# One-core hybrid-attention layer: in the last phase, the transposed copies of u and y of its last tiles made by DMA transposes instead of TensorE

## The chip, the cores and the metric

The kernel runs on one core of one Trainium2 chip. The metric is the device time of one execution in microseconds (us). The kernel before has a median of 2243.91 us over three runs. A core has TensorE (PE, matrix products), VectorE (DVE), ScalarE (ACT), GpSimd (POOL) and SyncE (SP), which issues nearly all the transfers (DMAs) of this kernel, in order.

## The reference

The reference is one layer of a streaming encoder: 2048 prompt rows and 8 running streams with 16 rows each (128 sample rows, with 512 cached positions). What matters here is the end of the layer.

```
h = rms_norm(x, g) * (1 + scale) + shift
qa, ka, va, za, qb, kb, vb, zb, ga, gb = split(h @ w_in)
oa = differential attention(qa, ka, va);  ob = stick-breaking attention(qb, kb, vb)
u  = [rms_norm(oa) * silu(za),  ob * silu(zb)]
y  = sigmoid(ga) * (u_a @ w_branch_a) + sigmoid(gb) * (u_b @ w_branch_b)
x  = x + gate * (y @ w_out)
out = rms_norm(x, final_g)
```

All matrices are 1024 wide (u_a and u_b 512 each). The gate is one row for the whole prompt and one row for each of the 8 sample streams.

## The kernel before

The rows are 17 tiles of 128: 16 of the prompt and one of the sample (number 16, `NT`). Every float32 operand of a product is split into a high and a low float16 part, and a product is the sum of three float16 products (high by high, high by low, low by high).

A first part normalizes x and projects, eight head units follow with their attention over all tiles, and the last phase computes u, y and the output tile by tile. The change touches the last phase alone. Its loop runs over slots n = 0 to 18, in the order `tiles` = 0 to 14, the sample, 15; places in this order are called indices here, so index 15 is the sample tile and index 16 the last prompt tile. In slot n the kernel emits:

- `branches` of index n: four pieces (two column halves, two branches) of 12 products each (L1463). DVE multiplies each result by its sigmoid gate (L1465) and adds the two branches (L1468); ACT and DVE write y as two float16 halves into the single buffer `y16` (L1469, L1470).
- `output` of index n-1: two halves of 24 products each with w_out (L1492). DVE scales by the gate (L1496), POOL adds to x (L1500). For the sample tile the gate rows are first loaded and spread over the partitions by a product (`gate_rows`, L1449 and L1451), and ACT and DVE scale (L1498, L1499).
- `inputs` of index n+2: loads (L1290, L1291, L1297), u, and its split into `u16`, which lies in `hs[2]` (L314, L319).
- `turned` of index n+1 and `turned_y` of index n: the products need u and y with their columns on the partitions. `transposed` does that: 16 transposes of 128x128 on TensorE (L1280) into two PSUM banks, and two copies to SBUF by ACT (L1281), one for each half.
- `normed_rows` and `stored_rows` of index n-2: the sum of squares (ACT, L294), the reciprocal root by ten small DVE operations (`rsqrt_one`, L273 to L286), the scaling by final_g (DVE, L1510) and the store (L1511).

Beside the first 13 slots (`S_TILES`) runs the attention of the sample tile (`sample`, `aside`), whose products with cached values are L871, with keys L848, and whose weights are already turned by DMA transposes (L614). A list of positions in each slot (`IN_AT`, and the numbers in `side`) and the costs of the pieces set where each piece is emitted; a scheduler then fixes the order on every engine. Cached values lie in the four buffers `dc`.

## Time and profile before

| | |
|---|---|
| Median of 3 runs | 2243.91 us (2241.89 to 2244.5) |
| Profiled execution, its own time | 2241.22 us |
| Its span | 2239.4 us |
| PE busy | 2082.9 us (93%) |
| DVE busy | 1749.2 us (78%) |
| ACT busy | 1621.5 us (72%) |
| POOL busy | 704.0 us (31%) |

The profile is of one execution. Its own time is 1.8 us above its span. Matmuls are pipelined, and their ends are modelled, so the time of one matmul in a chain is read from start to start and not from its duration. "L1280" is line 1280 of the kernel before. A row of the timeline has the start, the length, the engine, the line, the operation with its operands and count, and in brackets the idle time before it and what ended it. In the answers by stretches, each engine has its busy time and, in brackets, its number of instructions.

### The profile page before, as it was taken

The page shows a single profiled execution, that of the slowest core. Times are in us where ns is not written, and L with a number is a line of the kernel's source. Part 1 is how long each engine was busy: PE and PEld are TensorE (multiplying, and loading weights), DVE is VectorE, ACT ScalarE, POOL GpSimd, SP SyncE. Part 2 cuts the span into 40 slices and gives each one's busy share as a digit, 9 for nine tenths or more (in the row PEclk, how much of TensorE's full clock was granted, in tenths as well). Part 3 has the DMA queues.
Part 4 walks back from the last instruction along what each step waited for, and adds up shares of the span by engine and source line. Part 5 has one row for each costly group of instructions (what it writes and reads, how often), then busy time and mean ns, then how long its engine had stood idle before and what let it go on. Part 6 is the DMA issues. An engine that isn't in the chain of part 4 may idle for free.

```text
span 2239.4 us, 41736 instructions
## 1 busy us (share of the span) xinstructions
PE 2082.9 (93%) x14752; PEld 1127.2 (50%) x14752; DVE 1749.2 (78%) x3795; ACT 1621.5 (72%) x3228; POOL 704.0 (31%) x610
## 2 busy tenths in 40 slices
PE   5998999999999999999989998999998679999997
PEld 3654555555555555555555554555554334444543
DVE  4657868889886788988778888886688868788863
ACT  3967877789877677988677788866677665766641
POOL 1123014456410443742034365402234412212211
PEclk7999999999999999999999999999998799999999
DMA  9777668889796989979879899666677899999521
GB/s 331 266 238 184 165 152 212 196 221 205 197 247 160 224 201 201 213 205 225 200 197 211 182 234 223 170 157 136 140 157 158 183 259 255 235 255 240 158 101 57
DMA packets 805827, 445.30 MB, mean 199 GB/s; under 512 B 537354, under 2 KB 744506, under 8 KB 805104
## 3 DMA queue, kind: packets, MB, share of 16 engines
q1 hardware_dynamic: 804668, 442.24, 79.6%
q8 instruction: 115, 1.88, 0.3%
q14 instruction: 96, 0.79, 0.1%
q10 hardware_dynamic: 948, 0.39, 0.1%
HBM read 228.82 MB, written 86.02 MB: 141 GB/s over the span
## 4 chain that ended last, share of the span: by engine, by line
PE 31%; DVE 7%; ACT 5%; DMA 5%; issue 3%; POOL 1%; SPq 0%; DVEq 0%; POOLq 0%; ACTq 0%
PE ps_o L1492 7%; PE ps_mm L1463 7%; PE ps_mm L460 5%; PE ps_t L536 5%; DMA wt<-sc_n 2%; DVE sc_n L670 2%; PE ps_s L1280 1%; PE ps_s L697 1%; PE ps_s L696 1%; ACT sc_p L130 1%; POOL sc_p L676 1%; PE ps_o L757 1%; PE ps_t L871 1%; ACT sc_n L130 1%; DVE sc_n L607 1%
## 5 line engine op out<-in xcount | busy, mean ns | idle before, releaser
L676 POOL TENSOR_TENSOR sc_p<-sc_p,sc_n 128x127 f32<-128x127 f32 (+7 forms) x192 | 313.1, 1633 | 668.0 <-DVE sc_n L670 515.5
L460 PEld LDWEIGHTS <-hs 128*128 128x128 f16 x3120 | 292.6, 99 | 315.3 <-issue 6.7
L460 PE MATMUL ps_mm<-wa,hs 128*128 128x512 f16 x1590 | 383.3, 380 | 3.3 <-DMA hs<-hT_d 2.1
L460 PE MATMUL ps_mm<-wb,hs 128*128 128x512 f16 x1530 | 382.3, 381 | 0.2 <-DVE qbuf L495 0.2
L536 PE MATMUL ps_t<-wb,hs 128*128 128x512 f16 x1224 | 291.9, 379 | 3.2 <-DVE qst L564 2.9
L670 DVE TENSOR_TENSOR_SCAN sc_n<-ps_s,sc_n,zero_t 128x512 f32<-128x512 f32 x192 | 245.5, 1279 | 35.5 <-ACT ps_s L130 30.1
L696 PE MATMUL ps_s<-k,qst 128*128 128x512 f16 (+3 forms) x640 | 225.7, 354 | 33.5 <-DVE sc_n L670 24.8
L607 DVE TENSOR_TENSOR sc_n<-sc_p,sc_n 128x128 f16<-128x128 f32 (+7 forms) x192 | 221.9, 1158 | 40.0 <-ACT sc_n L604 39.5
L536 PEld LDWEIGHTS <-hs 128*128 128x128 f16 x1632 | 154.8, 98 | 182.2 <-DVE qst L564 7.3
L130 ACT ACTIVATE sc_p<-ps_s,usc 128x512 f32<-128x512 f32 (+3 forms) x320 | 202.9, 634 | 37.6 <-PE ps_s L697 23.0
L697 PE MATMUL ps_s<-k,qst 128*128 128x512 f16 (+3 forms) x640 | 226.1, 354 | 0.0
L604 ACT CAST sc_n<-sc_p 128x128 f16<-128x128 f32 (+7 forms) x192 | 154.8, 807 | 64.7 <-POOL sc_p L676 64.0
L130 ACT ACTIVATE ps_s<-ps_s,usc 128x512 f32<-128x512 f32 (+3 forms) x320 | 195.1, 610 | 0.0
L1492 PE MATMUL ps_o<-wo,wb 128*128 128x512 f16 x816 | 186.7, 385 | 0.7 <-ACT wb L1281 0.7
L757 PE MATMUL ps_o<-v,wt 128*128 128x128 f16 x1088 | 136.1, 227 | 21.8 <-DMA wt<-sc_n 21.8
L1500 POOL TENSOR_TENSOR x<-m,x 128x512 f32<-128x512 f32 x34 | 49.9, 1467 | 272.6 <-DVE m L1496 164.9
L590 DVE TENSOR_SCALAR_CACHE_REDUCE sc_p<-ps_s,usc 128x512 f32<-128x512 f32 (+3 forms) x160 | 106.3, 665 | 32.5 <-PE ps_s L697 18.6
L757 PEld LDWEIGHTS <-wt 128*128 128x128 f16 x1088 | 103.6, 102 | 50.0 <-DMA wt<-sc_n 27.0
L758 PE MATMUL ps_o<-v,wt 128*128 128x64 f16 x1088 | 128.6, 199 | 0.0
L1492 PEld LDWEIGHTS <-wb 128*128 128x128 f16 x816 | 79.6, 99 | 97.1 <-issue 4.6
L670 DVE TENSOR_TENSOR_SCAN sc_n<-ps_s,zero_t 128x128 f32<-128x128 f32 (+3 forms) x128 | 104.2, 815 | 22.9 <-ACT ps_s L130 22.1
L501 POOL TENSOR_TENSOR rot<-pr,rope 128x256 f32<-128x256 f32 x68 | 56.8, 835 | 203.8 <-ACT pr L474 115.1
(370 smaller groups left out, 4572.2 us busy)
## 6 DMA issues: line engine op xcount, KB each, us to landing
hs<-hT_d SPq DMA_DIRECT2D x130, 512.0 KB, 4.8
g_d<-gt SPq DMA_DIRECT2D x68, 256.0 KB, 3.1
out_dram<-pr SPq DMA_DIRECT2D x204, 64.0 KB, 3.6
wa<-in_w_in_dram SPq DMA_DIRECT2D x34, 256.0 KB, 5.3
o_d<-o SPq DMA_DIRECT2D x136, 64.0 KB, 2.0
wa<-g_d SPq DMA_DIRECT2D x17, 512.0 KB, 4.7
wb<-g_d SPq DMA_DIRECT2D x17, 512.0 KB, 4.8
hs<-o_d SPq DMA_DIRECT2D x17, 512.0 KB, 4.2
```

The source lines that it names most:

```text
L130: i = S.activation(**kw)
L460: T.matmul(box["p"], box["h"][:, hi, k, :], U["w"][k][:, wi, :], start=(n == 0), stop=(n == 3 * KT - 1))
L536: T.matmul(box["g"][:, 0:gw], box["h"][:, hi, k, :], U["wg"][k // per][:, k % per, wi, :], start=(j == 0), stop=(j == 3 * KT - 1))
L604: x = S.copy(out=hi, in_=src)
L607: V.tensor_tensor(out=lo, in0=src, in1=hi, op=ALU.subtract)
L670: V.tensor_tensor_scan(out=dst[:, lo : lo + n][:, ::-1], data0=src[:, 0:n][:, ::-1], data1=zero_t[:, 0:1].to_broadcast([P, n]), initial=fi ...
L676: G.tensor_tensor(out=p[:, 0:m], in0=p[:, 0:m], in1=n[:, 1 : m + 1], op=ALU.mult)
L696: T.matmul(p[:, 0:n], qst[:, c, :], kk[:, c, 0:n], start=True, stop=False)
L697: T.matmul(p[:, 0:n], qst[:, 2 + c, :], kk[:, c, 0:n], start=False, stop=not diag)
L757: T.matmul(po[:, c * P : (c + 1) * P], wt[:, wj, :], vt[:, c, :, :], start=first, stop=False)
L1463: T.matmul(pb, st["u"][:, ui * 8 + br * 4 + k, :], wb[br * 4 + k // 2 * 2 + j][:, wi, k % 2, :], start=(n == 0), stop=(n == 11))
L1492: T.matmul(po, st["y"][:, yi * 8 + k, :], wo[j * 4 + k // 2][:, wi, k % 2, :], start=(n == 0), stop=(n == 3 * KT - 1))
```

## The change

A constant `MOVED = 12` marks the indices from which the transposes move.

- u of indices 12 to 16 is turned by one DMA transpose from `u16` (SP issues it), instead of 16 TensorE transposes and two ACT copies.
- y of indices 12 to 15 is turned by one DMA transpose from `y16` into a new buffer `yT`, taken from the four `dc` buffers. It is emitted right after the last branch piece (position 4.4 in place of 7). y of index 16 is still turned by TensorE.
- The sample's gate rows are loaded once (9 x 1024) in slot 15, into a `dc` buffer, and the spreading product stands ahead of the products of each half.
- For the last tile, DVE in place of POOL adds to x, the sum of squares is taken by halves right after each half, and the scaling and the store are done by halves. In the last two slots the rows of index n-2 are normalized at earlier positions.

```diff
+MOVED = 12
...
-    def turned(st):
+    def turned(st, moved=False):
         st["u"] = st["u"].bitcast(F16).rearrange("p (k n) -> p k n", n=P)
+        if moved:
+            nc.sync.dma_start_transpose(out=st["u"], in_=st["u16"].rearrange("p f n -> p (f n)"))
+            return
         for half in range(2):
             transposed(st["u16"], st["u"], half)
...
+        def rows_of_gates():
+            L["gsm"] = dec.tile([P, NB, P], F32, tag="dc", name="gsm", bufs=4).rearrange("p b n -> p (b n)")
+            load(out=L["gsm"][0:9, :], in_=gate_d)
...
-        def turned_y(st):
+        def turned_y(st, moved):
+            if moved:
+                yT = dec.tile([P, NB, P], F32, tag="dc", name="yT", bufs=4).rearrange("p b n -> p (b n)")
+                st["y"] = yT = yT.bitcast(F16).rearrange("p (k n) -> p k n", n=P)
+                nc.sync.dma_start_transpose(out=yT, in_=L["y16"].bitcast(F16))
+                return
...
+                if t == NT:
+                    pg = bank("ts"[j])
+                    T.matmul(pg, sel[0:9, :], L["gsm"][0:9, c], start=True, stop=True)
...
-                    V.tensor_tensor(out=m, in0=m, in1=gate_rows(1, j), op=ALU.mult)
-                G.tensor_tensor(out=x[:, c], in0=m, in1=x[:, c], op=ALU.add)
+                    V.tensor_tensor(out=m, in0=m, in1=pg, op=ALU.mult)
+                if t != tiles[-1]:
+                    G.tensor_tensor(out=x[:, c], in0=m, in1=x[:, c], op=ALU.add)
+                    return
+                V.tensor_tensor(out=x[:, c], in0=m, in1=x[:, c], op=ALU.add)
+                if j == 0:
+                    box["acc"] = tiny.tile([P, 4], F32, tag="mx", name="facc")
+                sum_squares(x[:, c], 512, box["acc"][:, j : j + 1])
...
         def normed_rows(t, box):
+            if t == tiles[-1]:
+                return
...
+            if t == tiles[-1]:
+                r = rsqrt_one(add_up(box["acc"], 2), D, tiny, "rF")
+                for c in (slice(0, 512), slice(512, D)):
+                    V.scalar_tensor_tensor(out=x[:, c], in0=x[:, c], scalar=r, in1=fg[:, c], op0=ALU.mult, op1=ALU.mult)
+                    load(out=y_rows(t)[:, c], in_=x[:, c])
+                return
...
-                side += [(2, lambda n=n: turned(states[tiles[n + 1]])), ...
-            if n > 1:
+                side += [(2, lambda n=n: turned(states[tiles[n + 1]], n + 1 >= MOVED)), ...
+            if n <= NT and tiles[n] == NT:
+                side.append((3.3, rows_of_gates))
+            if n > NT:
+                side += [(0.6, lambda n=n: normed_rows(tiles[n - 2], boxes[n - 2])), (1.1, lambda n=n: stored_rows(tiles[n - 2], boxes[n - 2]))]
+            elif n > 1:
...
-                side.append((7, lambda n=n: turned_y(states[tiles[n]])))
+                side.append((4.4 if MOVED <= n < NT else 7, lambda n=n: turned_y(states[tiles[n]], MOVED <= n < NT)))
```

Ahead of slot 11 the order is the same on every engine. Three places are shown. The lines of the changed kernel are its own (L1298 there is L1297 before, L1346 the transpose of u, L1487 that of y).

The first is SP in slots 12 and 13, before: the gate loads (`g_d`, L1297), the store and load of x (L1511, L1485), and the loads for the inputs (L1290, L1291).

```order
L1297 DMA wa_175<-g_d_110 128x2x512
L1511 DMA out_dram<-x_26237 128x1024
L1291 DMA hs_181<-z_d_95 128x1024
L1485 DMA x_26866<-in_x_prompt_dram 128x1024
L1297 DMA wb_1428<-g_d_110 128x2x512
L747 DMA o_d_78<-o 128x128
L1290 DMA hs_180<-o_d_78 128x1024
L1291 DMA hs_181<-z_d_94 128x512
L1297 DMA wa_169<-g_d_112 128x2x512
```

The same place in the changed kernel:

```order
L1298 DMA wa_175<-g_d_110 128x2x512
L1541 DMA out_dram<-x_26216 128x1024
L1292 DMA hs_181<-z_d_95 128x1024
L1498 DMA x_26793<-in_x_prompt_dram 128x1024
L1298 DMA wb_1428<-g_d_110 128x2x512
L1487 DMA_TRANSPOSE yT<-wa_174 128x16x128
L1346 DMA_TRANSPOSE wb_1432<-hs_182 128x16x128
L748 DMA o_d_78<-o 128x128
L1291 DMA hs_180<-o_d_78 128x1024
L1292 DMA hs_181<-z_d_94 128x512
```

The two transposes stand right behind the second gate load, and ahead of the store of the sample's last head and the loads that follow it.

The second is DVE after the products of the sample's output, before: the sample's scaling (L1499), that of the last tile (L1496), and the start of the sample's reciprocal root.

```order
L1499 TENSOR_TENSOR m<-m,ps_t 128x512 x2
L1496 SCALAR_TENSOR_TENSOR m<-ps_o,fuy,gate 128x512 x2
L273 TENSOR_SCALAR r_27575<-facc 128x1
L276 TENSOR_SCALAR r_27575<-r_27575 128x1
L278 TENSOR_SCALAR rF<-r_27575 128x1
L280 SCALAR_TENSOR_TENSOR r_27575<-rF,r_27575 128x1
```

The same place in the changed kernel (L1512 is L1496 before, L1519 the new addition on DVE, L274 is L273 before):

```order
L1515 TENSOR_TENSOR m<-m,ps_t 128x512
L1515 TENSOR_TENSOR m<-m,ps_s 128x512
L1512 SCALAR_TENSOR_TENSOR m<-ps_o,fuy,gate 128x512
L1519 TENSOR_TENSOR x_27345<-m,x_27345 128x512
L274 TENSOR_SCALAR r_27381<-facc 128x1
L277 TENSOR_SCALAR r_27381<-r_27381 128x1
L1512 SCALAR_TENSOR_TENSOR m<-ps_o,fuy,gate 128x512
L279 TENSOR_SCALAR rF<-r_27381 128x1
L1519 TENSOR_TENSOR x_27345<-m,x_27345 128x512
L281 SCALAR_TENSOR_TENSOR r_27381<-rF,r_27381 128x1
```

The second half of the last tile now stands between the first operations of the sample's root.

The third is the end of DVE, before: the sample's last scaling, and then the last tile's root and scaling.

```order
L1510 SCALAR_TENSOR_TENSOR x_27426<-x_27426,rF,gt_1421 128x1024
L273 TENSOR_SCALAR r_27592<-facc 128x1
L276 TENSOR_SCALAR r_27592<-r_27592 128x1
L278 TENSOR_SCALAR rF<-r_27592 128x1
L280 SCALAR_TENSOR_TENSOR r_27592<-rF,r_27592 128x1
L281 TENSOR_SCALAR r_27592<-r_27592 128x1
L282 TENSOR_SCALAR r_27592<-r_27592 128x1
L283 TENSOR_TENSOR rF<-rF,r_27592 128x1
L284 SCALAR_TENSOR_TENSOR r_27592<-rF,r_27592 128x1
L285 TENSOR_SCALAR r_27592<-r_27592 128x1
L286 TENSOR_TENSOR rF<-rF,r_27592 128x1
L1510 SCALAR_TENSOR_TENSOR x_27514<-x_27514,rF,gt_1421 128x1024
```

The same place in the changed kernel:

```order
L277 TENSOR_SCALAR r_27427<-r_27427 128x1
L287 TENSOR_TENSOR rF<-rF,r_27381 128x1
L279 TENSOR_SCALAR rF<-r_27427 128x1
L1540 SCALAR_TENSOR_TENSOR x_27261<-x_27261,rF,gt_1421 128x1024
L281 SCALAR_TENSOR_TENSOR r_27427<-rF,r_27427 128x1
L282 TENSOR_SCALAR r_27427<-r_27427 128x1
L283 TENSOR_SCALAR r_27427<-r_27427 128x1
L284 TENSOR_TENSOR rF<-rF,r_27427 128x1
L285 SCALAR_TENSOR_TENSOR r_27427<-rF,r_27427 128x1
L286 TENSOR_SCALAR r_27427<-r_27427 128x1
L287 TENSOR_TENSOR rF<-rF,r_27427 128x1
L1536 SCALAR_TENSOR_TENSOR x_27345<-x_27345,rF,gt_1421 128x512 x2
```

Three operations of the last tile's root now stand ahead of the sample's scaling, and the last scaling is two halves.

On PE, 144 of the transposes of L1280 are gone from slots 11 to 16.

More of the change, by code (lines that the diff above doesn't have):

```diff
@@ L1543, in layer_kernel @@
             if n + 1 <= NT:
-                side += [(2, lambda n=n: turned(states[tiles[n + 1]])), (4.5, lambda n=n: opened(states[tiles[n + 1]]))]
-            if n > 1:
+                side += [(2, lambda n=n: turned(states[tiles[n + 1]], n + 1 >= MOVED)), (4.5, lambda n=n: opened(states[tiles[n + 1]]))]
+            if n <= NT and tiles[n] == NT:
[3 more added lines that the diff above has]
+            elif n > 1:
                 side += [(1, lambda n=n: normed_rows(tiles[n - 2], boxes[n - 2])), (2.5, lambda n=n: stored_rows(tiles[n - 2], boxes[n - 2]))]
             if n <= NT:
-                side.append((7, lambda n=n: turned_y(states[tiles[n]])))
-            order = [(i, 0, cost, fn) for i, (cost, fn) in enumerate(work)] + [(at - 0.5, i + 1, 0.9 if at in (2, 7) else 0.1, fn) for i, (at, fn) in enumerate(side)]
+                side.append((4.4 if MOVED <= n < NT else 7, lambda n=n: turned_y(states[tiles[n]], MOVED <= n < NT)))
+            order = [(i, 0, cost, fn) for i, (cost, fn) in enumerate(work)] + [(at - 0.5, i + 1, 0.9 if at == 7 or at == 2 and n + 1 < MOVED else 0.1, fn) for i, (at, fn) in enumerate(side)]
             work = [(cost, fn) for _, _, cost, fn in sorted(order, key=lambda e: e[:2])]
```

## Prediction

> **What bounds the kernel now.** I read the head of the page first, then the busy times in the stretches of the last slots (about one slot each), then TensorE's timeline.
>
> ```profile
> span 2239.4 us, 41736 instructions
> ...
> core 0: us, PE busy (x) PEld busy (x) DVE busy (x) ACT busy (x) POOL busy (x), PEclk, DMA share, GB/s
> 2100.00:2124.00 24.00, 24.00 (x222) 11.96 (x221) 18.19 (x39) 14.64 (x21) 5.60 (x5) 1.00 0.51 153
> 2124.00:2147.00 23.00, 23.00 (x140) 11.63 (x137) 14.89 (x32) 10.60 (x15) 4.87 (x3) 1.00 0.24 85
> 2147.00:2169.00 22.00, 22.00 (x123) 10.71 (x121) 15.92 (x42) 12.68 (x17) 3.81 (x3) 1.00 0.44 161
> 2169.00:2192.00 23.00, 23.00 (x139) 11.65 (x138) 11.50 (x23) 6.88 (x9) 2.53 (x2) 1.00 0.15 53
> 2192.00:2216.00 24.00, 23.27 (x124) 10.88 (x120) 9.49 (x21) 6.53 (x10) 2.01 (x2) 1.00 0.12 45
> 2216.00:2239.40 23.40, 11.69 (x50) 4.83 (x50) 8.72 (x25) 3.17 (x5) 4.30 (x4) 0.82 0.11 46
> ```
>
> TensorE is busy for the whole of each stretch up to 2192, at full clock, while DVE has 6 to 12 us to spare in each, ACT 9 to 16, and the transfer engines are busy for about half of their time or less. So in these slots the time is the sum of what TensorE does, and whatever leaves TensorE's list shortens the run, as long as nothing that it then needs comes late. Only the last stretch differs: its products end at 2227.7, and 11.7 us of other work follow.
>
> **The transposes that leave TensorE.** Its timeline, at two places with transposes (L1280) and at the last tile:
>
> ```profile
> 2168.94 1.06 PE L1280 MATMUL ps_s<-id,wa 128*128 128x128 f16 x16
> 2169.83 5.34 PE L1463 MATMUL ps_mm<-wa,wa 128*128 128x512 f16 x24
> ...
> 2182.60 9.01 PE L1492 MATMUL ps_o<-wo,wb 128*128 128x512 f16 x41
> 2191.45 1.06 PE L1280 MATMUL ps_s<-id,wa 128*128 128x128 f16 x16
> 2192.34 5.34 PE L1463 MATMUL ps_mm<-wa,wb 128*128 128x512 f16 x24
> ...
> 2213.06 0.22 PE L1280 MATMUL ps_s<-id,wa 128*128 128x128 f16 x1
> 2213.21 1.12 PE L1451 MATMUL ps_t<-gsm,sel 9*128 9x512 f32 x2
> 2214.26 1.01 PE L1280 MATMUL ps_s<-id,wa 128*128 128x128 f16 x15
> 2216.01 5.79 PE L1492 MATMUL ps_o<-wo,wb 128*128 128x512 f16 x26 [0.74 <-ACT wb L1281]
> 2221.73 1.12 PE L1451 MATMUL ps_t<-gsm,sel 9*128 9x512 f32 x2
> 2222.78 4.92 PE L1492 MATMUL ps_o<-wo,wb 128*128 128x512 f16 x22
> ```
>
> A group of 16 transposes takes from its start to the next start 2169.83 - 2168.94 = 0.89 us, and again 2192.34 - 2191.45 = 0.89. Five u (indices 12 to 16) and four y (12 to 15) are moved, nine groups: 9 x 0.89 = 8.0 us. All nine stand in slots 11 to 16, which the table covers but for slot 11, and there TensorE is never idle. Their 18 copies on ACT go too; ACT has room, so I count nothing for them.
>
> The Trainium skill (TensorE: Matmul & The Clock Gate, Part 4: PE-mode transpose) gives a transpose as about 275 ns in a kernel's context. By that, nine groups would be an estimated 39.6 us. The rows here have 56 ns from start to start, so the trace decides, and the sum has 8.0.
>
> **The transfers that replace them.** Transposes of the same make are in this kernel already. I take their rows from the page's list of transfers (count, median us from issue to landing), from the answer on their line (issue time on SP in ns, minimum, median, maximum, and the times to landing), and the rows around one y.
>
> ```profile
> wt<-sc_n SPq DMA_TRANSPOSE x288, 4.3
> dwt<-dsc SPq DMA_TRANSPOSE x12, 4.2
> ...
> L614 SPq DMA_TRANSPOSE wt<-sc_n x288: 1167/1765/5597, 149.5 to 1770.9; - x144
> DMA to landing us min/median/max: 2.3/4.3/7.6
> ...
> 2139.74 2.75 PE L1463 MATMUL ps_mm<-wb,wa 128*128 128x512 f16 x12
> 2145.64 0.69 DVE L1470 TENSOR_TENSOR wa<-wb,wa 128x512 f16<-128x512 f32 x1 [0.68 <-ACT wa L1469]
> 2146.65 0.53 SPq L1297 DMA_DIRECT2D wb<-g_d  x1
> 2151.80 0.32 SPq L1290 DMA_DIRECT2D hs<-o_d  x1
> ```
>
> A product of 512 columns takes (2191.45 - 2182.60) / 41 = 0.216 us. The tightest y is that of index 13. Its last branch product ends 12 x 0.216 = 2.6 us after 2139.74, at 2142.3, and its float16 halves are ready at 2146.3, 4.0 us later. In TensorE's new order, 15 output products of index 12 and 36 branch products of index 14 come between that last branch product and the first product that reads this y: 51 x 0.216 = 11.0 us. So 7.0 us are left. SP first issues the gate load that waits for the same DVE operation (0.53 us), and 6.5 us remain for a transfer that takes 4.3 in the median: on time by 2.2 us. The longest of the 288 rows, 7.6, would be late by 1.1. The other y have more (61 products instead of 51 for indices 12 and 14; about 14 us and an early y for 15). I take lateness 0, with 1.5 us as the upper end for all four together.
>
> The u are turned a whole slot before their use (some 21 us), and cost TensorE nothing. On SP, the nine issues take 9 x 1.8 = 16 us in all, spread over six slots. Queued behind a waiting y transpose are the store of the sample's last head and the loads of o, z and the next gates. Those feed u of the slot after the next: L1290 at 2151.80 loads what is multiplied one slot later. A delay of 2 to 4 us there is covered by that slot. The new wait of the next `y16` write (ACT) for the transfer to have read the buffer falls near the same 11 us, and holds up ACT and then DVE by a microsecond at most; two product banks are free of it.
>
> In slots 11 and 12 TensorE also serves the sample's attention, whose products wait for ACT, DVE and transfers. Two of the nine groups (u of 12 and 13) leave there. If that chain sets the pace, their 1.8 us return as waits. The new order puts output products ahead of the sample's products where the transposes were, so I take 0 here and 1.8 as the upper end.
>
> **The last tile.** The products of the sample's gate rows stay (1.05 us each, twice), only elsewhere. Before, the copy that TensorE waits for (L1281) stood behind ACT's L1498, which waited for the gate product: from 2213.06 to 2216.01 are 2.95 us, less 1.05 of gate product 1.9. After, it is 0.45 us for the first eight transposes, then ACT's L1498 (0.69) and one copy (1.0), 1.8 with the hops: 0.1 us gained. The work behind the last product is on these rows (the last two are times to landing, of the 512 KB store from the answer on x, and of the smallest store from the page).
>
> ```profile
> 2227.81 0.75 DVE L1496 SCALAR_TENSOR_TENSOR m<-ps_o,fuy,gate 128x512 f32<-128x512 f32 x1 [2.93 <-PE ps_o L1492]
> 2228.64 1.26 POOL L1500 TENSOR_TENSOR x<-m,x 128x512 f32<-128x512 f32 x1 [2.42 <-DVE r L273]
> 2229.93 1.06 ACT L294 ACTIVATE junk<-x 128x1024 f16<-128x1024 f32 x1 [3.78 <-POOL x L1500]
> 2230.90 0.19 ACT L294 ACTIVATION_READ_ACCUMULATOR junk<-x 128x1 f32 x1
> 2231.22 1.28 DVE L1510 SCALAR_TENSOR_TENSOR x<-x,rF,gt 128x1024 f32<-128x1024 f32 x1
> 2234.56 1.28 DVE L1510 SCALAR_TENSOR_TENSOR x<-x,rF,gt 128x1024 f32<-128x1024 f32 x1
> ...
> DMA to landing us min/median/max: 2.6/2.6/2.6
> ...
> o_d<-o SPq DMA_DIRECT2D x136, 64.0 KB, 2.0
> ```
>
> Before, the last scaling ends 2235.84 - 2227.7 = 8.1 us after the last product. DVE was held by the sample's root and scaling until 2231.22 + 1.28 = 2232.5, so the long way over POOL and ACT (to 2231.1) was hidden. After, DVE's order is: scaling (0.75), one step of the sample's root, the addition (0.7), then the sum of squares of half a tile on ACT (about 0.7 with reading, half of 1.06 plus 0.19), which ends 2.4 us after the last product. From there DVE still has the small sum, the rest of the sample's root mixed with the first three steps of the last (seven operations of 0.2, since ten of them lie between 2232.5 and 2234.56), the sample's scaling (1.2), seven steps (1.5) and two halves (1.4): 2.5 + 1.4 + 1.2 + 1.5 + 1.4 = 8.0. So the sample's scaling still lies on the path and almost nothing is gained there. The last store has half the size: between 2.0 and 2.6 us to landing, I take 2.3. Together 0.4 us, and between 1.0 lost (two stores and the sample's share the transfer engines) and 1.2 gained.
>
> **The sum.** 8.0 + 0.1 + 0.3 = 8.4 us off the profiled execution's 2241.22, which makes 2232.8. That execution is 2.7 us under the median of the runs (2243.91); on the median it is 2235.5. The ends: 8.4 - 1.5 (late y) - 1.0 (stores) = 5.9, and 8.4 + 0.9 = 9.3, so 2234.6 to 2238.0, and the runs shown lie 2.0 below to 0.6 above their median: 2232.5 to 2238.6.
>
> **The rivals.** One bound on what can be told: the measurement of this kernel separates about 0.2%, 4.5 us, from no change.
>
> *Partly given back.* The sample's chain keeps slots 11 and 12 at their length, and y of indices 13 and 14 come late. 8.4 - 1.8 - 1.5 - 1.0 = 4.1, 2239.8 on the median, at the border of what can be told. For it speaks that in the first stretch DVE is at 18.19 of 24 us, and that a gate load of 128 x 1024 values goes into the same queue right ahead of each y. Against it that the lateness needs the longest landing of 288, in slots where the transfers are far less busy than where those were taken.
>
> *TensorE was not the bound in these slots.* Then only the end moves, 0.4 us: 2243.5. Against it is the idle time of zero in five stretches.
>
> *Slower: y comes so late that the clock falls.* The place is the first product of `output` in slots 13 to 16. These rows of stretches show what a stall does to the clock (the column before the last two). Behind the last product, which ends at 2227.7, it is full up to 2231 and then half; after an earlier stall it is still half while TensorE is busy again for 4 us, and then full.
>
> ```profile
> 2230.00:2231.00 1.00, 0.00 (x0) 0.00 (x0) 0.85 (x5) 1.00 (x2) 0.00 (x0) 0.99 0.00 0
> 2231.00:2232.00 1.00, 0.00 (x0) 0.00 (x0) 0.94 (x2) 0.08 (x1) 0.00 (x0) 0.50 0.00 0
> ...
> 1776.00:1780.00 4.00, 3.75 (x31) 2.74 (x29) 3.22 (x9) 2.61 (x4) 1.58 (x2) 0.50 1.03 342
> 1780.00:1784.00 4.00, 4.00 (x19) 1.78 (x18) 3.96 (x9) 0.73 (x1) 2.33 (x1) 0.95 0.74 173
> ```
>
> A y late by 3.3 us costs 3.3 and about 2 more for 4 us at half clock, 5.3; four times 21, less 8.4: slower by 12.8, 2256.7. It decides from a mean lateness of 3.2 us for the four (12.9 us of waiting, to be 4.5 above before), so from landings of about 10 us for index 13 and more for the rest. Behind a gate load on the same transfer engines that could be; the longest of 288 is 7.6. The Trainium skill (TensorE: Matmul & The Clock Gate, Part 1) says that the clock halves after one idle window of 3.4 us and takes as long to return; this trace agrees, with the fall between 3.3 and 4.3 us after the last product.
>
> **How the numbers follow.** The forecast has 0.74, partly given back 0.12, not the bound 0.05, slower 0.09. The first is faster by over 0.2% (below 2239.4), the second in something over half of its cases: 0.81 faster. The rest of the second and the third make 0.10 within 0.2%, and 0.09 slower. The range is the forecast's ends and the partial case: the upper end at 2240.5, just over its 2239.8, the lower at 2231.5, 1 us below the forecast's own end, since the sum of start-to-start times has an error of that size.
>
> **What would show it.** Right: the chain of waits runs through PE without a gap from 2100 to the last product; only 32 starts of L1280 are left from slot 12 on; slots 13 to 15 are 1.8 us shorter each; the y transposes land 3 to 6 us after their issue; and the work behind the last product takes 11 to 12 us. Wrong: idle time at the first output product of a slot with a DMA named as what ended it, clock at 0.50 in slots 13 to 16, products with cached values (L871) waiting in slots 11 and 12, or over 12.5 us behind the last product.

## The result, and the profile after

The changed kernel has a median of 2236.94 us (2228.43 to 2245.64) over 22 runs, the kernel before 2243.8 (2235.05 to 2250.03) over 22 runs: a ratio of 0.997, with a 95% interval of 0.996 to 0.9981. That is 6.9 us less by the medians; 8.4 were forecast. The profiled execution took 2238.37 us (before 2241.22).

A line number of the changed kernel is one above that of before up to L1346. After it, the branch products are L1471 (L1463 before), the halves of y L1478, the output products L1508 (L1492), the scaling by the gate L1512 (L1496) and the scaling by final_g L1540. New are the transposes by transfer L1346 (u) and L1487 (y), for the sample tile the product of the gate rows L1503, and in the last tile DVE's addition L1519 and the scaling by halves L1536. The sample's products with cached values are L872.

The first fence has the busy times by stretch of the kernel before, now cut exactly at the slots 11 to 15 (a slot starts with the transposes of the y before it, or with its first branch product). The second has the same of the changed kernel.

```profile
2073.41:2099.24 25.83, 25.83 (x198) 12.90 (x194) 23.31 (x58) 17.33 (x26) 5.16 (x3) 1.00 0.52 170
2099.24:2123.93 24.69, 24.69 (x233) 12.53 (x230) 18.62 (x40) 15.40 (x22) 6.34 (x5) 1.00 0.51 154
2123.93:2146.43 22.50, 22.50 (x132) 11.15 (x130) 14.68 (x30) 10.37 (x14) 4.87 (x3) 1.00 0.25 88
2146.43:2168.94 22.51, 22.51 (x129) 11.19 (x128) 16.13 (x43) 12.85 (x19) 3.81 (x3) 1.00 0.43 157
2168.94:2191.45 22.51, 22.51 (x130) 11.16 (x129) 11.21 (x22) 6.94 (x9) 2.53 (x2) 1.00 0.16 55
```

```profile
span 2236.6 us, 41454 instructions
...
2077.31:2102.69 25.38, 25.38 (x181) 11.85 (x178) 22.80 (x59) 15.69 (x24) 5.23 (x3) 1.00 0.66 199
2102.69:2127.28 24.59, 24.04 (x216) 11.68 (x213) 19.58 (x41) 13.78 (x20) 6.85 (x5) 1.00 0.65 175
2127.28:2148.01 20.73, 20.73 (x101) 9.38 (x99) 12.53 (x30) 5.84 (x10) 4.88 (x3) 1.00 0.54 145
2148.01:2169.91 21.90, 20.89 (x97) 9.32 (x96) 16.80 (x43) 9.48 (x14) 4.25 (x3) 1.00 0.72 191
2169.91:2190.63 20.72, 20.72 (x97) 9.41 (x96) 11.02 (x22) 4.06 (x6) 2.54 (x2) 1.00 0.56 131
```

Slots 13 and 15 are 1.77 and 1.79 us shorter, two groups of transposes each. Slot 14 is only 0.61 shorter, and slots 11 and 12 together 0.55 instead of 1.78. In slots 12 and 14 PE's busy time is below the length. The chain of waits and PE's timeline name what it waited for:

```profile
PE ps_o L1508 <- DMA yT<-wa: 1.0, 1, 1.0
PE ps_o L1508 <- ACT wb L1282: 0.8, 1, 0.8
PE ps_t L872 <- DVE v16c L320: 0.5, 1, 0.5
...
2120.46 0.63 PE L872 MATMUL ps_t<-v16c,dwt 128*32 128x128 f16 x32
2121.59 0.41 PE L872 MATMUL ps_t<-v16c,dwt 128*32 128x128 f16 x16 [0.49 <-DVE v16c L320]
...
2153.19 2.75 PE L1471 MATMUL ps_mm<-wb,wb 128*128 128x512 f16 x12
2156.95 2.55 PE L1508 MATMUL ps_o<-wo,yT 128*128 128x512 f16 x11 [1.01 <-DMA yT<-wa]
...
2213.67 1.06 PE L1281 MATMUL ps_s<-id,wa 128*128 128x128 f16 x16
2215.51 10.53 PE L1508 MATMUL ps_o<-wo,wb 128*128 128x512 f16 x48 [0.79 <-ACT wb L1282]
```

The y of index 13 comes 1.01 us late in slot 14, and a half of the sample's values (L320) 0.49 late in slot 12. The answer on the buffer of the y transposes, and SP's rows around the late one, show why the first happens:

```profile
L1487 SPq DMA_TRANSPOSE yT<-wa x4: 3170/4192/5262, 2124.1 to 2186.4; - x4
...
DMA to landing us min/median/max: 6.1/6.3/6.5
...
2149.01 0.53 SPq L1298 DMA_DIRECT2D wb<-g_d  x1
2149.59 5.26 SPq L1487 DMA_TRANSPOSE yT<-wa  x1
```

The four transposes take 3.2 to 5.3 us to issue. A landing is on record for two of them only, those of indices 12 and 14 (6.1 and 6.5 us). The late one, of index 13, has none: from its issue at 2149.59 to the first product that reads it at 2156.95 are 7.4 us. The forecast had 1.8 and 4.3.

The end, on DVE:

```profile
2228.63 0.16 DVE L304 TENSOR_REDUCE col<-facc 128x1 f32<-128x2 f32 x1
...
2229.32 1.28 DVE L1540 SCALAR_TENSOR_TENSOR x<-x,rF,gt 128x1024 f32<-128x1024 f32 x1
...
2232.05 1.41 DVE L1536 SCALAR_TENSOR_TENSOR x<-x,rF,gt 128x512 f32<-128x512 f32 x2
```

The last product ends at 2215.51 + 10.53 = 2226.04 and the last scaling at 2233.46, 7.4 us behind it (8.1 before). From there to the end of the span are 3.1 us (before 2239.4 - 2235.84 = 3.6). Together 1.1 us are gained behind the last product.

All kernels are the same up to slot 11, but its start varies between 2073 and 2089 us from one execution to another, before any of the changed code. In the profile of the changed kernel it is 3.9 us later than in that of before, which is why these two executions differ by only 2.9 us. So differences below some microseconds are read from the slots, in this table (us). "Tail" runs from the first of the last tile's 48 output products to the end of the span (of before, less the gate product of 1.05 that lies in it). "Rest" is slot 16 up to there, less the gate products in it.

| kernel | slot 11 | 12 | 13 | 14 | 15 | rest | tail |
|---|---|---|---|---|---|---|---|
| before | 25.83 | 24.69 | 22.50 | 22.51 | 22.51 | 23.51 | 22.34 |
| changed | 25.38 | 24.59 | 20.73 | 21.90 | 20.72 | 22.78 | 21.09 |
| gates_late | 25.37 | 25.34 | 21.24 | 20.88 | 21.18 | | 21.09 |
| cost_kept | 24.94 | 26.13 | 20.72 | 21.63 | 20.72 | | 21.12 |
| rows_late12 | 25.37 | 25.60 | 21.18 | 22.59 | 20.73 | | 21.05 |
| sample_first | 25.37 | 25.67 | 20.72 | 22.69 | 20.72 | | 19.68 |
| y_halves | 25.37 | 24.33 | 20.72 | 20.72 | 20.72 | | 20.97 |
| y_queues | 25.37 | 24.41 | 24.97 | 20.72 | 20.72 | | 20.96 |
| rows_left | 25.38 | 25.49 | 20.73 | 21.53 | 20.77 | | 21.08 |
| u_from_14 | 26.18 | 25.51 | 20.73 | 21.54 | 22.18 | | 20.82 |
| product_left | 25.37 | 23.80 | 20.75 | 23.41 | 20.73 | | 21.05 |
| after_again | 25.38 | 25.19 | 20.72 | 24.54 | 20.71 | | 21.03 |
| best | 25.52 | 26.13 | 20.76 | 20.73 | 20.71 | | 19.64 |
| tail_only | 26.24 | 25.61 | 22.51 | 23.66 | 22.51 | | 20.99 |

Between before and changed the columns give 0.45 + 0.10 + 1.77 + 0.61 + 1.79 + 0.73 + 1.25 = 6.70 us.

### The profile page after: what moved, and what is told of

It reads as the page before. It is cut to its first block, busy times and chain, and to the rows that moved or that the text cites. A ratio compares the mean times of both kernels' runs of the same rounds, so it can differ in the third digit from the quotient of the medians.

```text
span 2236.6 us, 41454 instructions
## 1 busy us (share of the span) xinstructions
PE 2068.9 (93%) x14608; PEld 1115.8 (50%) x14608; DVE 1747.9 (78%) x3799; ACT 1606.9 (72%) x3212; POOL 700.4 (31%) x608
## 5 line engine op out<-in xcount | busy, mean ns | idle before, releaser
L677 POOL TENSOR_TENSOR sc_p<-sc_p,sc_n 128x127 f32<-128x127 f32 (+7 forms) x192 | 313.2, 1634 | 663.9 <-DVE sc_n L671 514.1
L608 DVE TENSOR_TENSOR sc_n<-sc_p,sc_n 128x128 f16<-128x128 f32 (+7 forms) x192 | 221.8, 1157 | 39.7 <-ACT sc_n L605 39.2
L758 PE MATMUL ps_o<-v,wt 128*128 128x128 f16 x1088 | 135.5, 226 | 22.5 <-DMA wt<-sc_n 22.5
L1508 PE MATMUL ps_o<-wo,wb 128*128 128x512 f16 x624 | 142.3, 384 | 0.8 <-ACT wb L1282 0.8
L754 PE MATMUL ps_o<-v,wt 128*128 128x128 f16 x544 | 101.5, 224 | 19.2 <-DMA wt<-sc_n 19.0
```

What stands on the lines that cost most here:

```text
L608: V.tensor_tensor(out=lo, in0=src, in1=hi, op=ALU.subtract)
L677: G.tensor_tensor(out=p[:, 0:m], in0=p[:, 0:m], in1=n[:, 1 : m + 1], op=ALU.mult)
L758: T.matmul(po[:, c * P : (c + 1) * P], wt[:, wj, :], vt[:, c, :, :], start=first, stop=False)
L1508: T.matmul(po, st["y"][:, yi * 8 + k, :], wo[j * 4 + k // 2][:, wi, k % 2, :], start=(n == 0), stop=(n == 3 * KT - 1))
```

## The experiments

Every edit is to the changed kernel. Three questions were open: what makes y late in slot 14, what keeps slots 11 and 12 long, and what the end is worth.

**Late y: the gate load ahead of it (gates_late).** The gates' load of the tile after the next is emitted behind the y transpose instead of ahead of it.

```
-                side += [(IN_AT[i], stage) for i, stage in enumerate(stages)]
+                side += [(4.45 if i == 6 and n >= MOVED else IN_AT[i], stage) for i, stage in enumerate(stages)]
```

> Same work as the changed kernel; on SP's queue the load of 512 KB of gates (L1298) stands behind the y transpose (L1487) instead of ahead of it, for indices 12 and on. Theory A (the y transpose takes 6.1 to 6.5 us to land because it queues behind that load, which shares its transfer engines): landing falls to 4.8 us or less, the 1.01 us that TensorE waits for yT in slot 14 is gone, the slot takes 20.7 us instead of 21.90. Theory B (it is the size of 16 blocks, whatever is ahead): landing stays at 5.8 us or more; the transpose is issued about 0.5 us earlier, so 0.5 us of the wait stay and the slot takes about 21.4. Slots 13 and 15 stay at 20.7 in both.

Measured 2242.87 us, one run beside 2248.92 of the kernel before. The answer on the transposes' buffer, and PE in slot 15:

```profile
L1487 SPq DMA_TRANSPOSE yT<-wa x4: 3170/3840/4342, 2128.1 to 2190.9; - x4
...
DMA to landing us min/median/max: 5.4/6.0/6.3
...
2179.58 0.61 PE L1508 MATMUL ps_o<-wo,yT 128*128 128x512 f16 x2 [0.29 <-DMA yT<-wa]
```

The three landings on record are those of indices 12 (6.3), 13 (6.0) and 14 (5.4). For index 13, 6.0 us stand against 7.4 from issue to first product in the changed kernel, and the transpose is issued 0.3 us after its y is written (L1478) instead of 0.9. Slot 14 loses its wait. But a wait of 0.29 for the y of index 14 appears in slot 15, and slot 13 loses 0.36: the load of o, now behind the moved gate load too, is issued 7.0 us into the slot instead of 5.5, and POOL (L1303), DVE (L1311, L1317) and then PE wait for it. So the load ahead decides the last microsecond, as far as one run shows; without it a whole transpose still takes 5.4 to 6.3 us, well over the 4.3 of the forecast.

**Late y: its size (y_halves, y_queues).** The transpose of 16 blocks becomes two of 8 blocks, both issued by SP; in y_queues ACT issues the second.

```
-                nc.sync.dma_start_transpose(out=yT, in_=L["y16"].bitcast(F16))
+                for h, queue in ((0, nc.sync), (1, nc.sync)):   # y_queues: (1, nc.scalar)
+                    queue.dma_start_transpose(out=yT[:, h * 8 : h * 8 + 8, :], in_=L["y16"].bitcast(F16)[:, h * D : h * D + D])
```

> Same work as the changed kernel; each y transpose of 16 blocks is issued as two of 8 blocks on SP, first the high half, which the first 16 of 24 products of each half tile read, then the low half. Theory A (the 6.1 to 6.5 us to landing, of which 3.2 to 5.3 are the issue itself, come from the size): each half is issued in 1.5 to 2.6 us, the first lands within 4.5 us of its issue, and the wait of about 1.0 us at the first output product of slot 14 (1.01, 0.73 and 1.80 in the runs so far with the gate load ahead) is gone; slot 14 takes 20.7 to 20.9 us. Theory B (a fixed cost of each transfer, or the load ahead of it): the first half lands after 5.5 us or more as the whole did, the second later still, and the wait stays near 1 us.

> Same work as the changed kernel; each y transpose is two of 8 blocks, the high half issued by SP and the low half by ACT's queue at the same time. Theory A (the issue on SP is what makes the landing long, and two queues share it): both halves land within 4.5 us, the wait in slot 14 is gone; ACT loses 1.5 to 2.5 us of its queue in each of slots 13 to 16, where it is busy for 5.8 to 9.5 of 21 us, at no cost. Theory B (the transfer engines make it long): the halves together take as long as one whole, 6 us, and the wait of 0.7 to 1.8 us stays; ACT's queue then holds the split of the next u by up to 4 us.

Measured 2248.57 and 2246.29 us, one run each, beside 2248.20 of before; slot 11 began 11.8 and 5.2 us later here than in the profile of the changed kernel, so the slots are compared. y_halves, its transposes and PE's first output products in slot 14:

```profile
L1488 SPq DMA_TRANSPOSE yT<-wa x8: 1233/1429/2312, 2134.3 to 2197.2; - x8
...
DMA to landing us min/median/max: 3.1/4.1/4.6
...
2164.69 2.54 PE L1509 MATMUL ps_o<-wo,yT 128*128 128x512 f16 x11
```

A half issues in 1.4 us in the median and lands in 4.1 (four of the eight landings are on record), and no y is late: slots 13 to 15 are 20.72 each, and slots 11 to the end take 157.7 us instead of 159.3. The scheduler also put the first half ahead of the gate load, so this is the size and the order together. In y_queues slot 14 is 20.72 too, but in slot 13 PE waits where a product bank is to be read:

```profile
2149.71 4.44 PE L1471 MATMUL ps_mm<-wb,wa 128*128 128x512 f16 x12 [2.41 <-DVE hs L1317]
```

The issue sits in ACT's own order, and what ACT and DVE do behind it comes later; slot 13 takes 24.97. Its 12 products take 4.44 us instead of 2.75: the granted clock was 0.50 for 3.4 us after this wait, of which more under after_again. The form is also not for use: the Trainium skill (DMA: Bandwidth & Descriptors, Silent corruption: two transposing streams in flight at once) warns that transposes issued from SP and from ACT can corrupt each other when they are in flight together. No run here shows that.

**Slots 11 and 12: order or chain (cost_kept, rows_late12, rows_left).** Three edits change what surrounds the sample's products. cost_kept gives the moved transposes the cost that the order was made with, rows_late12 moves the normalization of finished rows in slot 12 to the slot's end, and rows_left leaves the scaling of two tiles out.

```
-  0.9 if at == 7 or at == 2 and n + 1 < MOVED else 0.1
+  0.9 if at == 7 or at == 2 else 0.1                                   # cost_kept
-  side += [(1, ... normed_rows ...), (2.5, ... stored_rows ...)]
+  side += [(4.3 if n == MOVED else 1, ...), (4.6 if n == MOVED else 2.5, ...)]  # rows_late12
+            if t not in (MOVED - 3, MOVED - 2):                        # rows_left, ahead of root and scaling
```

> Same work as the changed kernel; the turning of u keeps its planned cost of 0.9 where transfers do it, so that in slot 11 the sample's products with cached values (L872, 28 of them) stand in one block again and not in three. Theory A (in slot 11 no wait took the gain: TensorE pays about 0.1 us at each change between these narrow products and the wide ones): slot 11 takes 24.9 to 25.0 us instead of 25.38, with no idle time on TensorE. Theory B (the sample's chain paces the slot): the products wait where they stand, and the slot keeps 25.4. Slot 12 stays at 24.6 with its 0.49 us wait for DVE's L320 in both.

> Same work as the changed kernel; in slot 12 alone the final normalization and the store of the tile before the last (L274 to L287, L1540, L1541; about 3.3 us of DVE) are planned for the end of the slot. Theory A (the cached-value products wait because DVE has its split of the values, L320, behind that normalization): the wait of 0.49 us at L872 is gone and slot 12 takes 24.0 us instead of 24.59. Theory B (the split is late because its data are late, by ACT's half or a transfer): the wait stays, and slot 12 keeps 24.5 or more.

> Leaves out the final normalization (ten steps of the root, the scaling: 3.3 us of DVE for a tile) of the two tiles stored in slots 11 and 12. TensorE's order is the same as in the changed kernel. Theory A (DVE, busy for 22.8 of 25.4 us in slot 11, paces slots 11 and 12 since the u transposes are gone; what the products wait for there follows from it): TensorE's idle time in slot 12 (0.55 to 1.7 us in the runs so far) goes, and slots 11 and 12 together take 49.2 to 49.5 us, against 50.52 before and 49.97 to 51.04 in four runs after. Theory B (the wait is for the transfers of the sample's weights, whose 10-block transposes are queued behind the new u transposes): the wait for dwt stays, and the two slots keep 50 to 51 us.

Measured 2240.44 and 2244.41 us (before 2248.92), and 2242.38 (before 2248.20), one run each. PE's rows of L872, cost_kept first (one block in slot 11, and slot 12), then rows_left in slot 12:

```profile
2082.15 0.84 PE L872 MATMUL ps_t<-v16c,dwt 128*32 128x256 f16 x24
...
2117.20 0.24 PE L872 MATMUL ps_t<-v16c,dwt 128*32 128x128 f16 x4 [1.06 <-DMA dwt<-dsc]
...
2123.93 0.41 PE L872 MATMUL ps_t<-v16c,dwt 128*32 128x128 f16 x16 [0.46 <-DVE v16c L320]
```

```profile
2119.82 0.24 PE L872 MATMUL ps_t<-v16c,dwt 128*32 128x128 f16 x4 [1.63 <-DMA dwt<-dsc]
...
2125.47 0.85 PE L872 MATMUL ps_t<-v16c,dwt 128*32 128x128 f16 x48
```

With the old cost, slot 11 is in full gain (24.94, 0.89 less than before: the sample's products are no longer cut in three), but slot 12 grows to 26.13, where both theories had 24.6, and the two take 51.07. With 6.6 us of DVE work left out, or with that work later, the wait for L320 goes, but a longer one for the sample's weights (`dwt`) takes its place: 50.87 and 50.97 for the two slots. The changed kernel had 49.97 in its first profile and 50.57 in a second (after_again, below): none of the three is shorter (all three have the late load of the next experiment, like after_again). So neither PE's order nor DVE's load sets this pace. It is a chain that ends in `dwt`.

**Is u of indices 12 and 13 worth moving (u_from_14)?** These two stay on TensorE.

```
-  turned(states[tiles[n + 1]], n + 1 >= MOVED)        and  at == 2 and n + 1 < MOVED
+  turned(states[tiles[n + 1]], n + 1 >= MOVED + 2)    and  at == 2 and n + 1 < MOVED + 2
```

> Same work as the changed kernel, but the u of indices 12 and 13 are turned by TensorE again (two groups of 16 transposes, 0.89 us each, in slots 11 and 12). Theory A (slots 11 and 12 are paced by DVE's chain, so that these two groups cost nothing): slots 11 and 12 together take 50.5 us, within 0.5 of the runs with the transfers (49.97 to 51.04). Theory B (TensorE is the bound there, as predicted): they take 51.7 us, 1.8 more than the changed kernel's 49.97.

Measured 2244.99 us, one run (before 2248.20). The two slots take 51.69, theory B's number. But they have to be compared at equal state of one transfer, the load of o in slot 11 (L1291): POOL's product that waits for it (L1303) starts 4.1 to 4.5 us after the load's issue in five of the profiles and 5.1 to 5.6 in nine, with or without the moved u, and with the late load the two slots are about 1 us longer. With the late load, u_from_14 has 51.69 and tail_only (below, u not moved either) 51.85; gates_late, rows_late12, sample_first, rows_left, after_again and best, with u moved, have 50.57 to 51.65, 50.97 in the mean. That is 0.8 less than the mean of those two. With the early load, before has 50.52, and the changed kernel, y_halves and y_queues 49.70 to 49.97: 0.55 to 0.82 less. So under half of the 1.78 us arrives.

**What the chain is (product_left).** POOL works in order. In slot 12 its gating product of index 14 (L1303) waits for the load of o, and behind it stands its part in the sample's weights (L677), behind which come ACT, DVE and the transposes into `dwt` (L615). This kernel leaves that one gating product out.

```
-            G.tensor_tensor(out=o[:, 0:nz], in0=o[:, 0:nz], in1=z[:, 0:nz], op=ALU.mult)
+            if t != tiles[MOVED + 2]: G.tensor_tensor(out=o[:, 0:nz], in0=o[:, 0:nz], in1=z[:, 0:nz], op=ALU.mult)
```

> Leaves out one product of the inputs, o by z of index 14 (L1303, 128 x 512 on POOL), that stands on POOL in slot 12 ahead of the sample's scan (L677). The orders of TensorE, DVE and SP are those of the changed kernel. Theory A (slot 12 is paced by the sample's chain: load of o, POOL's L1303 that waits for it, POOL's L677, ACT, DVE, the 10-block transposes of the weights dwt, the cached-value products): L677 begins about 2.4 us into the slot instead of 5.1 to 6.9, the transposes are issued about 1 us earlier against the load of o (7.7 us behind it instead of 8.7 to 8.95), the wait for dwt (0 to 1.6 us in the runs so far) is gone, and slot 12 takes 24.3 to 24.6 us with DVE's wait of up to 0.5 left. Theory B (the chain starts from DVE's second scan, so that POOL's wait is hidden): the issue comes as late as before and slot 12 keeps 24.4 to 25.7.

Measured 2243.41 us, one run (before 2250.94, median). POOL's timeline in slot 12 and a DVE row behind it (L608 prepares the weights for `dwt`), of the changed kernel, and then POOL's of this one, with this one's first L872 in slot 12 on PE:

```profile
2106.81 1.27 POOL L1303 TENSOR_TENSOR hs<-hs,hs 128x512 f32<-128x512 f32 x1 [2.16 <-DMA hs<-o_d]
2108.03 2.60 POOL L677 TENSOR_TENSOR dsc<-dsc 128x639 f32<-128x639 f32 x2
...
2110.15 1.16 DVE L608 TENSOR_TENSOR dsc<-dsc 128x640 f16<-128x640 f32 x1 [1.23 <-ACT dsc L605]
```

```profile
2109.31 1.31 POOL L677 TENSOR_TENSOR dsc<-dsc 128x639 f32<-128x639 f32 x1 [0.48 <-DVE dsc L671]
...
2119.00 0.24 PE L872 MATMUL ps_t<-v16c,dwt 128*32 128x128 f16 x4
```

L677 starts 2.3 us into the slot instead of 5.3. The weights' transposes are issued 7.7 us behind the load of o instead of 8.7, PE waits for nothing in slot 12, and the slot takes 23.80 us: 0.89 less than before, one group. That is less than the 24.3 to 24.6 that were expected with a wait for L320 left, and less than the 24.33 to 24.59 of the other three kernels with the early load and the moved u. The wait for L320 went too, since it hangs on the same chain: in the changed kernel DVE, in order, stood 1.23 us at L608 for weights that came late, and reached L320 17.6 us into the slot; here L608 waits for nothing, and L320 starts at 16.5. The load of o, POOL's order and the weights are the chain.

**The end (sample_first, tail_only).** In sample_first the sample's root and scaling stand ahead of the last tile's halves. tail_only takes the edits to the last tile and the gate rows alone, with all transposes on TensorE.

```
-  side += [(0.6, ... normed_rows ...), (1.1, ... stored_rows ...)]
+  side += [(0.3, ... normed_rows ...), (0.4, ... stored_rows ...)]     # sample_first
+  turned(..., False)   and   side.append((7, lambda n=n: turned_y(states[tiles[n]], False)))   # tail_only
```

> Same work as the changed kernel; in the last slot the sample tile's sum of squares, root, scaling and store are planned ahead of the last tile's first half, on ACT and DVE. Theory A (as predicted, the sample's root and scaling still lie between the last product and the end): DVE has 0.75 + 0.69 for the last half, ACT 0.82, then a sum and root of 2.3 and 1.41 of scaling, so the last scaling ends 6.2 us behind the last product's end instead of 7.6, and the whole tail from the last product's end takes about 9.4 us instead of 10.73. Theory B (the tail is paced by the stores or by the last tile's own steps): it stays within 0.3 us of 10.7.

> The changed kernel without its transfers: u and y of all indices are turned by TensorE as before, and only the last tile's edits stay (gate rows a slot ahead, sum of squares and scaling in halves). Theory A (nearly all of the gain is the 9 groups of transposes; the last tile's edits bring the 0.1 and 0.97 us that the traces show): slots 13 to 15 take 22.5 us each, the tail 10.7, and the whole is 1.1 us under the kernel before. Theory B (as predicted, 0.4 from the last tile): 0.4 under it. Theory C (the changed order of the work, not the transfers, moves the slots): slots 13 to 15 differ from 22.5.

sample_first measured 2246.23 us, one run (before 2248.92). Its last products on PE and the last scaling on DVE:

```profile
2224.72 10.53 PE L1508 MATMUL ps_o<-wo,wb 128*128 128x512 f16 x48 [0.79 <-ACT wb L1282]
...
2239.90 1.42 DVE L1536 SCALAR_TENSOR_TENSOR x<-x,rF,gt 128x512 f32<-128x512 f32 x2
```

The last scaling ends 6.1 us behind the last product (2235.25) instead of 7.4, and the tail is 1.4 shorter: the sample's scaling was on the path, as the prediction's sum has it. tail_only measured 2248.89 us over 11 runs, a ratio to before of 0.9993 (0.9982 to 1.0005), which by itself isn't told from no change. Its slots 13 and 15 are as before (slot 14 has a gate product in it), and its tail is 1.35 under that of before. By the slots, the last tile's edits bring a little over a microsecond, and the transfers the rest.

**Again, and the best of both (after_again, best).** after_again is the changed kernel unchanged, on the chip of the last runs; best has y in halves and the sample's scaling first.

```
y_halves + sample_first                                                 # best
```

> The changed kernel once more, as a base for the two others of this chip: about 6.9 us under the kernel before. Slots 13 and 15 take 20.7 us, slot 14 is 0.7 to 1.8 longer by the wait for yT, the tail from the last product's end takes 10.7.

> The changed kernel with y turned in two halves of 8 blocks and the sample's rows finished ahead of the last tile. From the slots of the single trials: slot 14 takes 20.7 us (0.7 to 2.0 less than in the changed kernel), the tail 1.4 less. Together 2.1 to 3.4 us under the changed kernel, so 9.0 to 10.3 us under the kernel before. If the gains didn't add (a rival: the earlier slot 14 only moves the wait into slots 15 and 16), it would be 1.4 under the changed kernel.

| | median of 12 runs | ratio to before (2250.94, 29 runs) |
|---|---|---|
| after_again | 2246.48 us (2242.24 to 2252.95) | 0.9982 (0.997 to 0.9993) |
| best | 2245.09 us (2236.56 to 2248.56) | 0.9971 (0.996 to 0.9983) |

On this chip the changed kernel is 4.5 us under before by the medians, where 6.9 were expected; the two intervals (0.997 to 0.9993 here, 0.996 to 0.9981 above) overlap. Best is 1.4 under the changed kernel, where 2.1 to 3.4 were expected; by the intervals, which overlap, it isn't told from it. By the slots it does what its parts did: slot 14 and the tail take 40.4 us, against 43.0 and 45.6 in the two profiles of the changed kernel. The 45.6 has an event of its own. PE's rows in slot 14 of after_again, and its stretches there (the column before the last two is the clock):

```profile
2159.13 3.63 PE L1508 MATMUL ps_o<-wo,yT 128*128 128x512 f16 x11 [1.96 <-DMA yT<-wa]
2162.55 3.40 PE L1471 MATMUL ps_mm<-wb,wb 128*128 128x512 f16 x12
...
2157.03:2160.44 3.41, 1.45 (x8) 0.61 (x8) 0.77 (x3) 1.28 (x3) 0.00 (x0) 1.00 0.93 232
2160.44:2163.85 3.41, 3.41 (x10) 1.17 (x9) 1.57 (x6) 1.76 (x2) 1.26 (x1) 0.50 1.06 209
2163.85:2167.26 3.41, 3.41 (x17) 1.56 (x16) 3.10 (x13) 1.06 (x1) 0.00 (x0) 1.00 0.37 135
```

The y is 1.96 us late, and then the clock is halved for 3.4 us: 11 and 12 products take 3.63 and 3.40 us instead of the 2.55 and 2.75 of the first profile. The slot is 3.8 us longer than one without a wait. This is the mechanism of the prediction's slower rival, at one place, in one execution. Of the 14 profiles one more shows it, that of y_queues in slot 13, behind its 2.41 us of waiting for L1317.

## Why the prediction was right or wrong

**Right: TensorE set the pace, and what leaves its list shortens the run.** Where nothing came late (slots 13 and 15), 16 transposes gave back 0.89 us, as the start-to-start rows said. tail_only, by its slots, shows that the transfers bring most of the gain. The rival by which TensorE was not the bound (2243.5) falls. Of the 8.4 us, 6.7 came by the slots: 1.2 less in slots 11 and 12, 1.2 less in slot 14, 0.3 less in slot 16 and 0.95 more in the tail. So the total is nearer to the forecast than its parts are, but without that surplus it would still lie in the stated range.

**Wrong size: the landing of y.** The step was a price of 4.3 us from the median of 288 transposes in this kernel, and lateness 0 in the sum. That median mixes sizes, and a landing is on record for few: 29 of the rows of L614. By the widths of the splits that feed them (L319 and L607, paired with L614 in order), 120 of the 288 have 16 blocks, as y has, and the others fewer. Those 120 took 2.8 us to issue in the median, and the 12 with a landing on record 4.2 to 7.6 to land, 5.2 in the median. In its place y took longer still. That of index 13 was issued 0.9 us after it was written and took 7.4 to its first product; 7.1 us were there in all, and it was 1.2 late. In the eight kernels that have this order and size, PE stood 0.6 to 2.4 us for it, 1.3 in the mean, with 6.5 to 7.8 us from issue to first product. The upper end of 1.5 covers the mean, not the longest. The load ahead (gates_late) and the size (y_halves) both count. This is the loss of 1.17 in slot 14. On SP the nine issues took 31.5 us instead of 16.

**Wrong size: slots 11 and 12.** The step was "I take 0 here and 1.8 as the upper end", because output products would fill the places of the transposes. Of 1.78 us 0.55 came. Over a third of the loss, 0.44 in slot 11, is no wait: the new order cuts the sample's products in three. The rest, 0.79 in slot 12, is the chain through POOL, which was not on the list. Its load of o also comes later with a u transpose right behind it: POOL's product starts 3.7 us after the load's issue in slot 12 of before, 4.2 to 4.4 in the ten kernels with the transpose there, 3.8 and 3.9 in u_from_14 and tail_only, where none stands behind it. The statement that a delay of this load "is covered by that slot" was about its reader on PE; POOL, in order, had the sample's weights behind it.

**Wrong size, to the good: the end.** 0.3 was forecast behind the last product in the sum (0.4 in the text ahead of it), 1.1 came. The sum was right in its form but for one term: the steps between the sum of squares and the sample's scaling took 0.69 us (2228.63 to 2229.32) instead of 1.4, since half of the sample's root had run while ACT squared. The smaller store gave 0.4, about as taken. The copy wait shrank from 1.9 to 1.84, where 0.1 was forecast.

**The rivals.** Of "partly given back", both losses came, at two thirds and three quarters of their price (1.2 of 1.8, 1.2 of 1.5); its third term, the stores, went the other way. So the result lies between the forecast's own ends and that rival. On the second chip the gain of 4.5 us is nearer to that rival's 4.1. The slower rival needs a mean lateness of 3.2 us over four places and got 1.3, nearly always at one place. Its clock falls from less than the 3.3 us of its price, though, as the last section shows.

Settled by the runs: size (with order) for the late y, the POOL chain for slot 12. That slot 11's missing 0.44 is the cut of the sample's products rests on the one run of cost_kept, and the POOL chain on the one run of product_left. Open: why the load of o in slot 11 comes a microsecond later in some executions.

## What to carry to other kernels

Before a transpose moves from TensorE to a transfer, price the transfer by its own size and its own place in the queue, and give each consumer's slack beside it; where the slack is short, two halves may be in time where one whole is late. Where a slot loses work on its busiest engine, look for the in-order queue (here POOL's) in which work for a second chain stands behind a wait for a load. The end of a kernel is summed operation by operation on its last engine; what runs while another engine finishes is not on that sum.

## What the runs showed of the hardware

**The cost of a transposing transfer grows with its size, that of its issue most.** From SBUF to SBUF, y as 16 blocks of 128x128 in float16 took 3.1 to 5.8 us to issue on SP over all runs, 4.2 in the median, and 5.4 to 7.3 to land where a landing is on record. As 8 blocks it took 1.2 to 2.3 and 3.1 to 5.4.

**The clock falls by the idle time within one step of a 3.41 us grid.** In all 14 profiles every change of the granted clock lies on a grid with this step, which lies differently in each execution. At full clock, each of the 193 steps with over 2.0 us without products (as the profile has them) was followed by half clock, 56 of the 206 steps with 1.5 to 2.0 us, and one of some 8200 with less; the clock came back at the end of every step with under 0.5 us. In after_again the 1.96 us fall into one step (1.45 of 3.41 busy, above). In product_left a longer wait of 2.35 us lies across two, and the clock stays:

```profile
2157.04:2160.45 3.41, 2.60 (x12) 0.97 (x10) 2.62 (x3) 0.99 (x2) 0.00 (x0) 1.00 1.23 201
2160.45:2163.86 3.41, 1.87 (x9) 0.90 (x10) 1.19 (x2) 1.83 (x3) 0.00 (x0) 1.00 1.08 253
```

So whether a wait of about 2 us costs as much again is a matter of where it falls. The Trainium skill (TensorE: Matmul & The Clock Gate, Part 1) speaks of an idle window of 3.4 us; the step agrees with it, but here some 2 us without products in one step were enough.

**DVE and POOL slow each other.** Rows of DVE and then of POOL, in sample_first, and then in y_halves, where the load of o landed earlier:

```profile
2092.03 3.58 DVE L320 SCALAR_TENSOR_TENSOR v16c<-dc,s_c,v16c 128x1024 f16<-128x1024 f32 x2 [0.51 <-ACT v16c L315]
...
2092.06 1.27 POOL L1303 TENSOR_TENSOR hs<-hs,hs 128x512 f32<-128x512 f32 x1 [2.29 <-DMA hs<-o_d]
```

```profile
2096.28 2.48 DVE L320 SCALAR_TENSOR_TENSOR v16c<-dc,s_c,v16c 128x1024 f16<-128x1024 f32 x2 [0.51 <-ACT v16c L315]
...
2095.20 1.27 POOL L1303 TENSOR_TENSOR hs<-hs,hs 128x512 f32<-128x512 f32 x1 [1.17 <-DMA hs<-o_d]
```

The same pair on DVE takes 1.1 us longer when POOL's operation starts beside it. In rows_late12, where DVE started 0.07 us ahead of POOL, POOL's operation took 2.34 us instead of 1.27. The Trainium skill (SBUF — State Buffer, SBUF: two separate sides) has a port pair of the two that one of them holds for a whole instruction; 1.1 us is about the length of POOL's operation, so the trace agrees.
